# Reading the bank of product 7 at its own product, and holding back the first loads

## The chip, the cores and the metric

The kernel runs on one core of a Trainium2 chip. The metric is the device time of one execution in microseconds (us). Before the change it is 2088.18 us, the median of 3 runs (2087.85 to 2088.67). The engines are called by the profile's names: PE (matrix multiply, with PEld for its weight loads), DVE (vector), ACT (scalar), POOL (GpSimd) and SP (which here only issues DMA transfers; "SPq" is its queue).

## The reference

One layer of a streaming encoder, for a prompt of 2048 tokens and a sample of 32 tokens that share the weights. Cut to what matters here:

```python
def layer(x, pool_hist, n_valid, S0, ...):
    h = rmsnorm(x, g_pre_mix)
    z = h @ w_in                                  # 1024 -> 2560 columns
    u, zq, zf, zi, zg = jnp.split(z, [...], axis=-1)
    ...                                           # pooling mixer and gated recurrence
    x = x + rmsnorm(y_mix, g_post_mix)
    h2 = rmsnorm(x, g_pre_ffn)
    f = (jax.nn.silu(h2 @ w_gate) * (h2 @ w_up)) @ w_down   # 1024 -> 2816 -> 1024
    return x + rmsnorm(f, g_post_ffn), new_pool, S1
```

The changed places are the very first product, `zi = h @ w_in[:, COL_I:]` of the first half of the prompt (the "values"), and the two products with `w_gate` and `w_up`.

## The kernel before, in words

The prompt is worked in two halves of 1024 tokens (`halves`). Every float32 operand of a large product is split into a rounded part "hi" and a rest "lo", and a product is three matmuls (hi*hi, hi*lo, lo*hi) of 128 x 128 weights with 512 columns; all of them are issued by line 199.

**The start.** `first_values` (line 566) runs with all engines in written order. The contraction over 1024 channels is cut into 8 blocks k of 128. For each block two things are loaded: the channels of x (tile `xT`, 128 x 512 floats, 256 KB per block) and the rows of `w_in` (tile `wrow`, 256 KB per block). Both come through SP's one queue, in the order of the code: x of block 0 in two halves around w 0, then w 1, x 1, then x 2 and 3 as one transfer (512 KB), w 2 and 3 as one, and so on to block 7, then the constants (`cons`), four token tiles `xt` of 512 KB (line 451), and more. Nothing holds these issues back but the queue itself. ACT and DVE split each block: ACT `xg` (line 600) and DVE `xg` (601) for x, ACT `whw` (612, 615, 236) and DVE `wlw` (614, 616, 237) for w; then PE does 12 matmuls for the block into four banks `vps`. Behind block 5 PE does the matmuls `rb<-dg` that spread the scale of the tokens; `dg` comes from the four token tiles through ACT (line 319, sum of squares), POOL (325, 326) and DVE (461).

**Gate and up.** `gate_up` (1246) computes the two products block by block in seven products of a Winograd-like 2 x 2 scheme (`step`, 1353). For each m (even: a block of `w_gate`, odd: one of `w_up`; 22 in each half) there are two accumulation banks: `M.x` takes products 1, 6, 5, 3 and `M.y` takes products 7 and 4. So product 4 adds into the bank that product 7 has filled, and the quantity c22 needs `M.y` as it stands after 7 and before 4, and `M.x` as it stands after 5 and before 3. ACT copies `M.x` into c22 behind product 5 (line 1393; for m = 4 and 5, which are not "held", DVE adds, line 1395), and `rest` (1402), run at the start of the next slot, has DVE add `M.y` (line 1403). `order_of` gives the slots: mostly (m,1), (m-1,4), (m-1,3), (m,6), (m,2), (m,7), (m,5); for the last two, a and b, it ends (a,7), (b,7), (a,5), (b,5), (a,4), (b,4), (a,3), (b,3). The weights are prepared some slots ahead (`advance`, 1431), and `hidden` (1201) splits finished results and stores them.

Then comes the product with `w_down` (`down`), whose tail ends the program.

Of the kernel before, what the change touches and what calls it, by code (L numbers as in the profile page):

```python
# [13 lines left out]
ALU = mybir.AluOpType  # L14
PSUM = bass.MemoryType.PSUM

P = 128
# [61 lines left out]
def body(tc, ins, outs, cst):  # L79
    nc = tc.nc  # L80
    ctx = ExitStack()
    with ctx:
# [9 lines left out]
        def ztile(name, shape=None, dt=F32):  # L92
            return UP.tile(shape or [P, SLOT], dt, tag="u", name=name)
# [13 lines left out]
        def t2(name, shape=None, dt=F32):  # L107
            return TP.tile(shape or [P, 512], dt, tag="t", name=name)
# [7 lines left out]
        x_t = ins["x_channels"].rearrange("(k p) t -> p k t", p=P)  # L116
        w_in = ins["w_in"][0]
# [154 lines left out]
        def raws(n):  # L272
            its = Stream.items
            while Stream.nraw < min(n, len(its)):
                its[Stream.nraw] = its[Stream.nraw]()
                Stream.nraw += 1
# [146 lines left out]
        COL_Q, COL_F, COL_I, COL_G = 512, 1024, 1536, 2048  # L423
# [19 lines left out]
        def channel_load(S, tg, k, n):  # L443
            t0 = S.tok0 + tg * 512
            nc.sync.dma_start(out=S.xT[tg][k // 2][:, k % 2:k % 2 + n], in_=x_t[:, k:k + n, t0:t0 + 512])
# [52 lines left out]
        def scaled_channels(S, tg):  # L498
            if S.B:
                rb = S.rb[tg]  # L500
            else:
                rb = axbank("rb")
                for i in range(4):
                    mm(rb[:, i * P:(i + 1) * P], ones, S.dg[tg][:, i], True, True, 112.0)
            if S.hT is None:
                S.hT = [(xtile(f"hThi{k}"), xtile(f"hTlo{k}")) for k in range(KD)]
            cs = slice(tg * 512, tg * 512 + 512)
            yield 0.0
            for k in range(0, KD, 2):
                x = S.xT[tg][k // 2]  # L510
                for i in range(2):
                    nc.vector.scalar_tensor_tensor(x[:, i], x[:, i], g_pre[:, k + i:k + i + 1], rb, ALU.mult, ALU.mult)
                    nc.scalar.copy(S.hT[k + i][0][:, cs], x[:, i])
                for i in range(2):
                    hi, lo = (t[:, cs] for t in S.hT[k + i])
                    nc.vector.tensor_tensor(lo, x[:, i], hi.bitcast(F32), ALU.subtract)
                S.seen[tg] = k + 2
                if S.B and tg == 0 and k >= 4:
                    ahead(Stream.used + k // 2 - 1)
                yield 5000.0 if S.B and tg == 0 else 2800.0  # L520
# [45 lines left out]
        def first_values(S):  # L566
# [7 lines left out]
            front_loads(S)  # L574
            S.xT[0] = [ztile("xT", [P, 2, 512]) for _ in range(4)]
            for kp in range(4):
                if kp:
                    channel_load(S, 0, 2 * kp, 2)
                    raws(kp + 1)
                    continue  # L580
                x0 = x_t[:, 0, S.tok0:S.tok0 + 512]
                nc.sync.dma_start(out=S.xT[0][0][:, 0, 0:256], in_=x0[:, 0:256])
                raw = ztile("wrow", [P, 2 * 512])
                Stream.items[0] = lambda: raw
                for i in range(2):
                    nc.sync.dma_start(out=raw[:, i * 512:(i + 1) * 512], in_=w_in[i * P:(i + 1) * P, COL_I:COL_I + 512])
                    if i == 0:
                        nc.sync.dma_start(out=S.xT[0][0][:, 0, 256:512], in_=x0[:, 256:512])
                    else:
                        channel_load(S, 0, 1, 1)  # L590
                raws(1)
# [18 lines left out]
            raw = Stream.items[0]  # L610
# [12 lines left out]
            for k in range(0, KD, 2):  # L623
# [9 lines left out]
                for kk in range(2):  # L633
# [9 lines left out]
                    if k + kk == KD - 3:  # L643
                        later = scaled_channels(S, 1)
# [601 lines left out]
        def gate_up(S, on_last):  # L1246
# [8 lines left out]
            jobs, later, gs = [], [], {}  # L1255
# [55 lines left out]
            def product(M, p, ps, start):  # L1311
                while p not in S.F:
                    S.post[1].step()
                wf, F = M.f.pop(p), S.F[p]
                for k in (0, 2):
                    trios = [(*(wf[:, i, kk * P:(kk + 1) * P] for i in range(2)),
                              *(x[:, (kk % 2) * 512:(kk % 2) * 512 + 512] for x in F[kk // 2])) for kk in (k, k + 1)]
                    for n, (a, b) in enumerate(in_turn(trios)):
                        mm(ps, a, b, start and k == 0 and n == 0, k == 2 and n == 5, rcost(512), not start)
                        if n % 3 == 2:  # L1320
                            poll()

            def close(M, name):
                c = getattr(M, name)
                if M.gate is None:
                    later.append(lambda: nc.scalar.activation(c, c, AF.Silu))
                else:
                    nc.vector.tensor_tensor(c, c, getattr(M.gate, name), ALU.mult)
# [24 lines left out]
            def step(m, p):  # L1353
                M = mats[m]
                if p == 1:
                    M.gate = mats[m - 1] if m % 2 else None
                    M.x = mmbank("gx") if M.held else axbank("gw")
                    product(M, 1, M.x, True)
                    M.c11 = t2("c11")
                    nc.scalar.copy(M.c11, M.x)  # L1360
                    if not M.held:
                        M.p1, M.c11 = M.c11, t2("c11")
                elif p == 2:
                    if M.held:
                        z = axbank("gz")
                        product(M, 2, z, True)
                        nc.vector.tensor_tensor(M.c11, z, M.c11, ALU.add)
                        close(M, "c11")
                    else:
                        product(M, 2, M.x, False)  # L1370
                        if M.gate is None:
                            nc.scalar.activation(M.c11, M.x, AF.Silu)
                        else:
                            nc.vector.tensor_tensor(M.c11, M.x, M.gate.c11, ALU.mult)
                elif p == 6:
                    if not M.held:
                        M.x = mmbank("gx")
                    product(M, 6, M.x, not M.held)
                    M.c21 = t2("c21")
                    if M.held:  # L1380
                        nc.scalar.copy(M.c21, M.x)
                    else:
                        nc.vector.tensor_tensor(M.c21, M.x, M.p1, ALU.add)
                    if m == len(mats) - 1:
                        sampled([m - 1, m])
                elif p == 7:
                    M.y = axbank("gy")
                    product(M, 7, M.y, True)
                elif p == 5:
                    product(M, 5, M.x, False)  # L1390
                    M.c22 = t2("c22")
                    if M.held:
                        nc.scalar.copy(M.c22, M.x)
                    else:
                        nc.vector.tensor_tensor(M.c22, M.x, M.p1, ALU.add)
                    if m < LEAD:
                        if m % 2:
                            sampled([m - 1, m])
                    elif m < len(mats) - 2 and m % 2 == 0:
                        sampled([m, m + 1])  # L1400

                    def rest():
                        nc.vector.tensor_tensor(M.c22, M.y, M.c22, ALU.add)  # L1403
                        close(M, "c22")
                    later.append(rest)
                elif p == 4:
                    product(M, 4, M.y, False)
                    nc.vector.tensor_tensor(M.c21, M.y, M.c21, ALU.add)
                    close(M, "c21")
                else:  # L1410
                    product(M, 3, M.x, False)
                    M.c12 = t2("c12")
                    src = M.x
                    if not M.held:
                        src = M.c12
                        nc.vector.tensor_tensor(M.c12, M.x, M.p1, ALU.add)
                        M.p1 = None
                    if M.gate is None:
                        nc.scalar.activation(M.c12, src, AF.Silu)
                    else:  # L1420
                        nc.vector.tensor_tensor(M.c12, src, M.gate.c12, ALU.mult)
                        jobs.append(hidden(S, m // 2, [M.c11, M.c12, M.c21, M.c22]))
                        mats[m - 1] = mats[m] = None
# [62 lines left out]
        class Down:  # L1486
            w = [None] * len(GROUPS)
# [308 lines left out]
```

## Time and profile before

| | before |
|---|---|
| median of 3 runs | 2088.18 us |
| profiled execution, its own time | 2086.21 us |
| its span, first to last instruction | 2084.4 us |
| PE busy | 2071.4 us (99%) |
| DVE, ACT, POOL busy | 68%, 40%, 14% |
| granted TensorE clock (mean of the core) | 0.998 |

The span is what the profile's rows cover; the profiled execution's own time is 1.8 us longer. A row of the timeline reads: start and length in us, engine, line, operation, tile written <- tiles read, shape, how many were merged, and in brackets how long the engine had been idle and what ended that.

### The profile page before, as it was taken

Reading aid. Unit: us, or ns where it says so; the run is one execution under the profiler, and the core shown is the slowest. Engines: PE = TensorE matmul, PEld = TensorE weight load, DVE = VectorE, ACT = ScalarE, POOL = GpSimd, SP = SyncE. Lnnn points to the kernel's source line nnn. Section 1 sums busy time; section 2 is a strip of 40 time slices with the busy share of each in tenths; the row PEclk is TensorE's granted clock in tenths of the full one; section 3 lists DMA queues with packets and bytes.
Section 4 is the critical chain, followed back from the end, with each engine's and each line's share of the span. In section 5 each row is a group of like instructions: output and inputs, shape, how many; then the busy total and the mean of one; then the engine's idle time right before and its main releaser. Section 6 shows DMA issues by size and latency. Waiting matters only on the chain.

```text
span 2084.4 us, 34134 instructions
## 1 busy us (share of the span) xinstructions
PE 2071.4 (99%) x13112; PEld 1689.0 (81%) x13112; DVE 1423.6 (68%) x2303; ACT 830.7 (40%) x1661; POOL 281.9 (14%) x387
## 2 busy tenths in 40 slices
PE   9999999999999999999999999999999999999998
PEld 8788888888888888788888788888888778888876
DVE  6566765787776778365575697776666766566587
ACT  6444445654444445233334563444444521011032
POOL 1133302100000000122231200000000210110133
PEclk9999999999999999999999999999999999999999
DMA  9321144435555558211014614554445796776778
GB/s 326 112 72 52 45 142 144 150 115 174 157 162 147 158 171 262 72 46 36 25 54 174 202 50 138 163 149 144 142 138 171 237 326 208 216 225 207 213 225 213
DMA packets 393361, 321.06 MB, mean 154 GB/s; under 512 B 18128, under 2 KB 320720, under 8 KB 393200
## 3 DMA queue, kind: packets, MB, share of 16 engines
q1 hardware_dynamic: 390752, 310.98, 48.1%
q0 software_dynamic: 2016, 7.34, 1.9%
q8 instruction: 103, 1.69, 0.3%
q10 hardware_dynamic: 432, 0.57, 0.1%
q14 instruction: 58, 0.48, 0.1%
HBM read 218.36 MB, written 100.47 MB: 153 GB/s over the span
## 4 chain that ended last, share of the span: by engine, by line
PE 94%; DVE 3%; issue 1%; ACT 1%; DMA 0%; POOL 0%; SPq 0%; DVEq 0%; POOLq 0%; ACTq 0%
PE gx L199 22%; PE mmb L199 16%; PE gy L199 11%; PE dx L199 10%; PE ops L199 10%; PE gz L199 5%; PE dy L199 5%; PE vps L199 4%; PE dz L199 3%; PE gb L199 1%; PE gw L199 1%; PE gsps L199 1%; DVE acc L1581 1%; PE ups L199 1%; PE tps L342 1%
## 5 line engine op out<-in xcount | busy, mean ns | idle before, releaser
L199 PE MATMUL gx<-fhi,wf 128*128 128x512 f32 x1376 | 387.0, 391 | 0.0
L199 PEld LDWEIGHTS gx<-fhi,wf 128*128 128x128 f32 x1376 | 256.7, 188 | 55.0 <-issue 2.2
L199 PE MATMUL gx<-flo,wf 128*128 128x512 f32 x688 | 213.1, 390 | 0.0
L199 PE MATMUL gy<-fhi,wf 128*128 128x512 f32 x704 | 201.6, 390 | 1.0 <-DVE c L1403 1.0
L199 PE MATMUL dx<-dhi,hst 128*128 128x512 f32 x640 | 185.3, 391 | 1.0 <-DVE acc L1581 0.9
L199 PE MATMUL mmb<-hTlo,whi 128*128 128x512 f32 x512 | 176.3, 405 | 0.0
L199 PE MATMUL mmb<-hThi,whi 128*128 128x512 f32 x512 | 165.8, 405 | 0.0
L1581 DVE TENSOR_TENSOR acc<-dx,acc 128x512 f32<-128x512 f32 x168 | 115.0, 689 | 71.3 <-PE dx L199 70.3
L199 PE MATMUL mmb<-hThi,wlo 128*128 128x512 f32 x512 | 159.0, 392 | 0.0
L1301 DVE TENSOR_TENSOR wf<-s,wf 128x512 fp32r<-128x512 f32 x176 | 119.7, 687 | 56.1 <-ACT wf L1296 54.2
L199 PEld LDWEIGHTS gy<-fhi,wf 128*128 128x128 f32 x704 | 131.8, 188 | 29.1 <-DVE c L1403 1.4
L199 PEld LDWEIGHTS gx<-flo,wf 128*128 128x128 f32 x688 | 129.1, 188 | 27.0
L1296 ACT CAST wf<-s 128x512 fp32r<-128x512 f32 x176 | 107.9, 621 | 102.3 <-DVE s L1277 31.5
L199 PEld LDWEIGHTS dx<-dhi,hst 128*128 128x128 f32 x640 | 119.6, 188 | 30.2 <-issue 3.4
L1520 ACT CAST dhi<-t 128x1024 fp32r<-128x1024 f32 x20 | 20.7, 1053 | 250.7 <-DVE dlo L1521 182.4
L1301 DVE TENSOR_TENSOR wf<-wraw,wf 128x512 fp32r<-128x512 f32 x132 | 89.6, 686 | 34.4 <-ACT wf L1296 34.4
L199 PEld LDWEIGHTS mmb<-hTlo,whi 128*128 128x128 f32 x512 | 96.2, 188 | 20.8 <-issue 1.3
L199 PEld LDWEIGHTS mmb<-hThi,wlo 128*128 128x128 f32 x512 | 96.3, 188 | 19.3 <-issue 0.7
L1296 ACT CAST wf<-wraw 128x512 fp32r<-128x512 f32 x132 | 80.7, 621 | 76.0 <-PE gx L199 36.3
L199 PEld LDWEIGHTS mmb<-hThi,whi 128*128 128x128 f32 x512 | 91.8, 188 | 21.1 <-issue 3.8
L199 PE MATMUL gy<-flo,wf 128*128 128x512 f32 x352 | 108.7, 389 | 0.0
L199 PE MATMUL dx<-dlo,hst 128*128 128x512 f32 x320 | 98.7, 389 | 0.0
(333 smaller groups left out, 3995.0 us busy)
## 6 DMA issues: line engine op xcount, KB each, us to landing
hst<-hdFalse SPq DMA_DIRECT2D x140, 256.0 KB, 2.9
hst<-hdTrue SPq DMA_DIRECT2D x140, 256.0 KB, 2.9
wraw<-in_w_gate_dram SPq DMA_DIRECT2D x50, 512.0 KB, 4.0
wraw<-in_w_up_dram SPq DMA_DIRECT2D x50, 512.0 KB, 4.0
hdFalse<-hhi SPq DMA_DIRECT2D x77, 256.0 KB, 2.3
hdFalse<-hlo SPq DMA_DIRECT2D x77, 256.0 KB, 2.3
hdTrue<-hhi SPq DMA_DIRECT2D x77, 256.0 KB, 2.6
hdTrue<-hlo SPq DMA_DIRECT2D x77, 256.0 KB, 2.6
```

The lines of the kernel that those rows point to most:

```text
L199: nc.tensor.matmul(out, l, r, start=start, stop=stop, skip_group_check=more)
L342: nc.tensor.transpose(ps[:, c:c + P], xn[:, (2 * kp + kk) * P:(2 * kp + kk + 1) * P], ident)
L1296: nc.scalar.copy(wf[:, 0], getattr(M, src) if isinstance(src, str) else src)
L1301: nc.vector.tensor_tensor(wf[:, 1], getattr(M, src) if isinstance(src, str) else src, wf[:, 0].bitcast(F32), ALU.subtract)
L1520: nc.scalar.copy(hi, src)
L1581: nc.vector.tensor_tensor(dst, ps, dst, ALU.add)
```

## The change

Two edits that do not touch each other. At the start the loads of block pairs are held back: x 2 and w 2, and x 3 and w 3, become four transfers of 256 KB. Before x 2 is issued, POOL copies one column of w 0 into the place that x 2 will fill, so that the transfer has to wait until w 0 has landed and POOL has run; before x 3 it does so from w 1; and before x 4 and 5 from x 1. All stand in SP's one queue, so what is behind them waits too.

In `step` the bank `M.y` is read into c22 at product 7 (ACT copy, or DVE add for m = 4 and 5), and at product 5 DVE adds `M.x` to it. `rest` is gone; only `close` (activation or multiplication) is left for the next slot.

```diff
             for kp in range(4):
+                if kp == 1:
+
+                    raw = ztile("wrow", [P, 2 * 512])
+                    Stream.items[1] = lambda: raw
+                    seen = Stream.items[0][:, 0:1], Stream.items[0][:, 512:513]
+                    for i in range(2):
+                        x, w = S.xT[0][1][:, i], raw[:, i * 512:(i + 1) * 512]
+                        nc.gpsimd.tensor_copy(x[:, 0:1], seen[i])
+                        nc.sync.dma_start(out=x, in_=x_t[:, 2 + i, S.tok0:S.tok0 + 512])
+                        nc.sync.dma_start(out=w, in_=w_in[(2 + i) * P:(3 + i) * P, COL_I:COL_I + 512])
+                    raws(2)
+                    continue
                 if kp:
+                    if kp == 2:
+                        nc.gpsimd.tensor_copy(S.xT[0][2][:, 0, 0:1], S.xT[0][0][:, 1, 0:1])
                     channel_load(S, 0, 2 * kp, 2)
                     raws(kp + 1)
                     continue
@@
                 elif p == 7:
                     M.y = axbank("gy")
                     product(M, 7, M.y, True)
+                    M.c22 = t2("c22")
+                    if M.held:
+                        nc.scalar.copy(M.c22, M.y)
+                    else:
+                        nc.vector.tensor_tensor(M.c22, M.y, M.p1, ALU.add)
                 elif p == 5:
                     product(M, 5, M.x, False)
-                    M.c22 = t2("c22")
-                    if M.held:
-                        nc.scalar.copy(M.c22, M.x)
-                    else:
-                        nc.vector.tensor_tensor(M.c22, M.x, M.p1, ALU.add)
+                    nc.vector.tensor_tensor(M.c22, M.x, M.c22, ALU.add)
...
-
-                    def rest():
-                        nc.vector.tensor_tensor(M.c22, M.y, M.c22, ALU.add)
-                        close(M, "c22")
-                    later.append(rest)
+                    later.append(lambda: close(M, "c22"))
```

## Rows read from the trace of the kernel before

**Rows 1.** The page, busy time, share of the span and instructions of each engine.

```profile
PE 2071.4 (99%) x13112; PEld 1689.0 (81%) x13112; DVE 1423.6 (68%) x2303; ACT 830.7 (40%) x1661; POOL 281.9 (14%) x387
```

**Rows 2.** Waits of PE, whole span: us in total, times, longest.

```profile
PE gy L199 <- DVE c L1403: 1.0, 1, 1.0
PE dx L199 <- DVE acc L1581: 0.9, 2, 0.7
```

**Rows 3.** Busy time by stage: stretch, length, busy us (instructions) of each engine.

```profile
5.26:8.98 3.72, 3.40 (x12) 2.48 (x12) 1.77 (x4) 1.70 (x3) 0.00 (x0) 1.00 0.92 289
8.98:9.77 0.79, 0.73 (x2) 0.30 (x2) 0.74 (x1) 0.11 (x1) 0.00 (x0) 1.00 1.07 412
...
384.00:770.00 386.00, 386.00 (x1720) 319.34 (x1719) 298.68 (x463) 187.63 (x326) 6.41 (x12) 1.00 0.50 148
1190.00:1640.00 450.00, 449.02 (x2623) 370.33 (x2622) 333.72 (x518) 208.02 (x369) 20.87 (x20) 1.00 0.48 144
```

**Rows 4.** The chain that ended last, first 60 us: start, us, what.

```profile
2.58 5.61 DMA xT<-x_channels
...
9.77 13.56 PE vps L199 x58
...
24.52 24.50 PE vps L199 x108
```

**Rows 5.** Timeline near the end of gate and up, second half.

```profile
1625.65 0.57 ACT L1393 COPY c<-gx 128x512 f32<-128x512 f32 x1
...
1628.06 0.63 PE L199 MATMUL gx<-fhi,wf 128*128 128x512 f32 x2
...
1628.94 0.68 DVE L1403 TENSOR_TENSOR c<-gy,c 128x512 f32<-128x512 f32 x1
...
1629.67 0.73 PE L199 MATMUL gy<-fhi,wf 128*128 128x512 f32 x2 [0.98 <-DVE c L1403]
```

**Rows 6.** Groups by line: count, busy us, mean ns, idle before and who ended it.

```profile
L199 PE MATMUL gx<-fhi,wf 128*128 128x512 f32 x1376 | 387.0, 391 | 0.0
...
L1403 DVE TENSOR_TENSOR c<-gy,c 128x512 f32<-128x512 f32 x44 | 30.3, 688 | 26.8 <-ACT c L1393 26.7
```

**Rows 7.** Timeline of the first 17 us, ACT, PE and SP.

```profile
1.17 0.42 SPq L586 DMA_DIRECT2D wrow<-in_w_in_dram  x1
...
5.26 2.48 PE L199 MATMUL vps<-whw,xg 128*128 128x512 f32 x8
...
6.07 0.62 ACT L615 CAST whw<-wrow 128x512 fp32r<-128x512 f32 x1 [0.45 <-DMA wrow<-in_w_in_dram]
...
8.21 0.72 ACT L600 ACTIVATE xg<-xT,cons 128x512 fp32r<-128x512 f32 x1 [1.52 <-DMA xT<-x_channels]
...
9.66 0.72 ACT L600 ACTIVATE xg<-xT,cons 128x512 fp32r<-128x512 f32 x1 [0.73 <-DMA xT<-x_channels]
...
16.13 1.14 ACT L236 CAST whw<-wrow 128x512 fp32r<-128x512 f32 x2 [0.23 <-DMA wrow<-in_w_in_dram]
```

**Rows 8.** DMA issues: count, KB each, median us to landing (first 1.5 us; whole span).

```profile
wrow<-in_w_in_dram SPq DMA_DIRECT2D x1, 256.0 KB, 3.4
...
hst<-hdFalse SPq DMA_DIRECT2D x140, 256.0 KB, 2.9
```

**Rows 9.** Timeline, one POOL operation without and with DVE at work beside it.

```profile
23.11 0.55 POOL L326 TENSOR_TENSOR st<-st,nhalf 128x1 f32<-128x1 f32 x1
...
2067.59 1.42 DVE L1612 SCALAR_TENSOR_TENSOR acc<-acc,st,gv 128x512 f32<-128x512 f32 x2 [0.57 <-POOL st L326]
...
2068.55 0.86 POOL L326 TENSOR_TENSOR st<-st,nhalf 128x1 f32<-128x1 f32 x1
```

**Rows 10.** Timeline, from the token tiles to the matmuls behind block 5.

```profile
21.60 1.06 ACT L319 ACTIVATE junk<-xt 128x1024 bf16<-128x1024 f32 x1
...
23.69 0.29 DVE L461 TENSOR_SCALAR dg<-cons,st 128x128 f32<-128x128 f32 x1 [0.96 <-POOL st L326]
...
24.03 0.30 PEld L199 LDWEIGHTS rb<-dg,ones 128*128 128x128 f32 x2 [0.23 <-DVE dg L461]
```

## The prediction

> **What bounds the kernel now.** I read the page's busy times first, then the waits of PE, then a table by stage, then the start and the one stall of gate and up in the timeline. PE is busy 2071.4 of 2084.4 us [rows 1], so an edit can only pay where PE stands still: 13 us in all. The waits of PE show how little of that has a name: one wait of 1.0 us on DVE's line 1403, and two on line 1581 in the product with `w_down` (0.9 us, not touched) [rows 2]. By stage, the first half's gate and up has PE busy 386.00 of 386.00 us and the second half's 449.02 of 450.00 [rows 3]: there the missing 0.98 us is that one wait. Whatever the first edit does to DVE and ACT elsewhere, PE has nothing to gain from it there. In the start, the chain that ends last runs through the landing of x 1 (2.58 + 5.61 = 8.19 us), then PE alone from 9.77 [rows 4]. So there are two places, about 1 us each.
>
> **Gate and up.** Per block m, nothing is added or removed: before, one ACT copy (of `M.x`, at product 5) and one DVE add (of `M.y`, one slot later); after, one ACT copy (of `M.y`, at product 7) and one DVE add (of `M.x`, at product 5). The DVE add stands at the same place in DVE's order, since nothing is issued between the end of a slot's step and the start of the next. What moves is who holds which bank. Before, product 4 could not start into `M.y` until DVE's add, late in DVE's queue, had read it; after, until ACT's copy, issued two or more slots earlier, has.
>
> The stall: the last gx matmul before it starts at 1628.06 + 0.63 - 0.39 = 1628.30 (two merged, one lasts 0.39 [rows 6]), the next, product 4 of a, at 1629.67, after line 1403 ran 1628.94 to 1629.62 [rows 5]. That is 1.37 us, where a matmul follows the one before it in 24.50 / 108 = 0.227 us [rows 4]: 1.14 us lost, of which 0.98 counts as idle. The slots just ahead of it are (a,7), (b,7), (a,5), (b,5). ACT's copies for a and b now belong to the first two, and ACT had come as far as the copy of (a,5) by 1625.65 [rows 5], so both would be done some 2 us before 1628.5. I take all of it: **-1.1 us**. Bounds: 0 if ACT is late after all, and +0.6 if ACT's copy, 0.57 us, came in front of a weight cast that PE waits for. What is late next: product 3 into `M.x` now waits for the DVE add instead of an ACT copy, but two slots of 12 x 0.227 = 2.7 us lie between. In the other 43 blocks the edit also ends a DVE wait on the ACT copy (26.7 us in all [rows 6]); it costs nothing now, because PE was busy throughout, and returns nothing. c22 is taken from its pool a slot earlier; a wait for a free buffer would stall ACT's copy, and the weights are prepared four slots ahead (10.9 us of PE), which I count as cover: 0.
>
> **The start, what the wait costs now.** From 5.26 to 9.77 PE starts 14 matmuls [rows 3]; at 0.227 us they need 3.18 us, so 4.51 - 3.18 = 1.33 us are lost. Of these, 0.5 are in the first eight (2.48 us instead of 7 x 0.227 + 0.39 = 1.98 [rows 7]), which no transfer held up. The other 0.8 us are block 1: ACT waited 1.52 us for x 1 [rows 7]. w 0 lands at 1.17 + 3.4 = 4.57 [rows 7, 8], before any held-back transfer could have moved, so the first matmul at 5.26 stays where it is.
>
> **What holding back does.** x 1 was issued at 2.58 and took 5.61 us, against 2.9 for 256 KB at the median [rows 4, 8]. If all its excess is the company of the 512 KB transfers behind it, it lands near 6.3; if none, at 8.19. I take 7: then ACT's `xg` of block 1 is no longer late and PE runs through from 5.26, 0.8 us ahead of before.
>
> POOL's copy of one column: the trace has no such copy. Its bounds are 0 and 0.55 us, the longer one-column operation [rows 9]; I take 0.2. Then x 2 is issued at about 4.57 + 0.3 = 4.9 (before: right behind x 1) and lands at 4.9 + 2.9 = 7.8, w 2 half a microsecond of issue later at 8.3. Before, x 2 and 3 landed at 9.66 and PE still had work; so blocks 2 and 3 are in time. SP has nothing else queued that anyone waits for soon. POOL's next work is the token statistics, past 19 us.
>
> But PE cannot keep the 0.8 us by itself. Behind block 5 it meets `rb<-dg`, and there it already waits 0.23 us for the last `dg` [rows 10]. That `dg` hangs on the last token tile (ACT 21.60, DVE 23.69), ACT's work before that on the landing of w 6 and 7 at 16.1, where ACT waited [rows 7], and that on every byte queued before it: from 8.98 us the transfers run at 412 GB/s with every DMA engine busy (share 1.07 [rows 3]). So the start gains only what the whole stream gains. Before, the stream ran at 289 GB/s from 5.26 to 8.98 [rows 3]: 3.72 x (1 - 289/412) = 1.1 us lost. After, that loss may shrink, but a gap is added, from x 1's end to the first bytes of x 2 at about 4.9 + 2.9 - 0.65 = 7.1 (256 KB at 412 GB/s are 0.65). With x 1 at 6.3 the gap is 0.8 and the net gain 0.3; with x 1 at 8.19 there is neither. I take **-0.3 us**; bounds -0.8 (PE's share) and +1.6 (rival 2).
>
> On the price of a gate the row and a page meet. The row: 2.9 us from issue to landing for 256 KB, of which 0.65 are bytes, so 2.2 are paid whenever nothing is queued ahead [rows 8]. The Trainium skill, "DMA: Bandwidth & Descriptors", section "Anatomy of one DMA — SWDGE (gpsimd) path", gives a fixed 2.0 us plus bytes at 436 GB/s for transfers issued from GpSimd, which makes 2.6 us as an estimate; the trace, of one issued from SP, agrees within 0.3. By the page the first bytes of x 2 come at 6.9 instead of 7.1, and the sum would be -1.6. The rule speaks against the change: each gate exposes a fixed part that a full queue had hidden.
>
> A second rule could lengthen the gate. The same one-column POOL operation takes 0.55 us, and 0.86 where DVE runs an operation with two SBUF inputs beside it [rows 9]. The Trainium skill, "SBUF — State Buffer", section "SBUF: two separate sides", says that these two share a port pair which one of them holds for a whole instruction. The trace agrees in sign; here it would add about 0.3 us to the first gate, and the sum would be -1.1.
>
> **The sum.** -1.1 - 0.3 = -1.4 us. The profiled execution's own time is 2086.21 (span 2084.4 and 1.8 around it); it becomes 2084.8. The median of the runs shown is 2.0 above the profiled one, so the forecast there is 2088.18 - 1.4 = 2086.8.
>
> **Rivals.** (1) Holding back does not do what it says: x 1 is late by itself, by its own packets, and lands near 8.2 as before. For it: ACT waited for w 1 too, until 6.07 [rows 7], when little of the later load can have moved. Against it: x 1 took twice as long as an ordinary 256 KB. The start gives 0, the sum -1.1: 2087.1.
> (2) Slower: the gates starve the stream. Place: the third gate, x 4 and 5 behind x 1. If x 1 lands at 8.19, POOL runs after a DVE operation (0.7, half of 1.42 [rows 9]) and takes 0.2, the issue is at 9.1 and its first bytes at 11.3, while what is queued (x 2 to w 3, 4 x 0.65 = 2.6 us from 8.2) ends at 10.8: 0.5 us idle, and a second slow stretch like the 289 GB/s one costs its 1.1 again. Then w 6 and 7, the last `dg` and PE are 1.6 us later: -1.1 + 1.6 = +0.5, 2088.7. It decides the sign from a delay of 1.1 us on.
> (3) The wait in gate and up is replaced, not removed: ACT's copy of `M.y` sits behind ACT's backlog and product 4 waits for it just as long. Against it: ACT was 2 us ahead there. Only the start is left: -0.3, 2087.9.
>
> **How the numbers follow.** Forecast 50%, rival 1 23%, rival 2 15%, rival 3 12%. The times lie between 2086.8 and 2088.7; the forecast's own bound on the start (-0.8) reaches 2086.3. With the spread of the runs shown (0.8 us) and the unknown costs (+0.6 in gate and up) the range is 2085.4 to 2089.0. A measurement of this kernel tells 0.2%, 4.2 us, from no change. No case reaches it: 4.2 us faster would take a third of all PE idle time, and 4.2 slower a stall that no row suggests, such as a wait for buffers. I leave 3% to each, 94% to within 0.2%.
>
> **What would show it.** Right: PE's waits no longer name the add of c22, and second-half gate and up is busy to the last 0.1 us; ACT's `xg` of block 1 starts by about 7 us; the wait at `rb<-dg` grows from 0.23 to about 0.7, because PE comes earlier than `dg` does. Wrong: ACT still waits for x 1 until 8 us (rival 1); w 6 and 7 land past 17 us and `rb` starts past 25 (rival 2); product 4 near the end waits for ACT (rival 3); any new wait of PE in gate and up.

## The result, and the profile after

| | before | after |
|---|---|---|
| median of 22 runs each | 2087.86 us | 2091.20 us |
| range of the runs | 2085.81 to 2090.14 | 2087.82 to 2093.64 |
| profiled execution, its own time | 2086.21 us | 2090.33 us |
| its span | 2084.4 us | 2088.4 us |

The change makes the kernel slower: ratio 1.0016, 95% interval [1.001, 1.0022], some 3.3 us. That lies above the range of the prediction (2085.4 to 2089.0), though inside the 0.2% that was called no change.

First the waits of PE in the changed kernel, the view of [rows 2] (us in total, times, longest):

```profile
PE rb L199 <- DVE dg L461: 2.4, 3, 1.0
...
PE gb L199 <- ACT f_t L879: 0.8, 3, 0.4
PE vps L199 <- ACT va L714: 0.6, 1, 0.6
```

The wait for c22 is gone. Two stand there that were not in the list before: `rb<-dg` at the start, 2.4 us in three waits, and `vps<-va` in the second half (`gb<-f_t` was there, with 0.5 us). The prediction had let the last wait at `rb<-dg` grow from 0.23 to 0.7, but at no cost, since PE was to come earlier; `vps<-va` it did not have.

Next the start. The timeline of the changed kernel, ACT, POOL and SP (answers to [rows 7] and [rows 9]):

```profile
4.62 0.18 POOL L584 COPY xT<-wrow 128x1 f32<-128x1 f32 x1 [3.62 <-DMA wrow<-in_w_in_dram]
4.83 0.33 SPq L585 DMA_DIRECT2D xT<-x_channels  x1
...
6.03 0.75 POOL L584 COPY xT<-wrow 128x1 f32<-128x1 f32 x1 [1.23 <-DMA wrow<-in_w_in_dram]
6.05 0.68 DVE L628 TENSOR_TENSOR wlw<-wrow,whw 128x512 fp32r<-128x512 f32 x1
6.63 0.72 ACT L614 ACTIVATE xg<-xT,cons 128x512 fp32r<-128x512 f32 x1
...
6.71 0.67 POOL L591 COPY xT<-xT 128x1 f32<-128x1 f32 x1
6.80 0.33 SPq L585 DMA_DIRECT2D xT<-x_channels  x1
...
7.71 0.38 SPq L445 DMA_DIRECT2D xT<-x_channels  x1
...
17.73 0.62 ACT L236 CAST whw<-wrow 128x512 fp32r<-128x512 f32 x1 [0.21 <-DMA wrow<-in_w_in_dram]
...
23.43 1.06 ACT L319 ACTIVATE junk<-xt 128x1024 bf16<-128x1024 f32 x1 [0.29 <-DMA xt<-in_x_prompt_dram]
...
25.52 0.29 DVE L461 TENSOR_SCALAR dg<-cons,st 128x128 f32<-128x128 f32 x1 [1.15 <-POOL st L326]
...
25.86 0.50 PEld L199 LDWEIGHTS rb<-dg,ones 128*128 128x128 f32 x2 [1.14 <-DVE dg L461]
```

Read it from the top. Gate one opens at 4.8. ACT's `xg` of block 1 starts at 6.63 with no wait, where it stood until 8.21 before: x 1 was indeed held up by its company, the 512 KB transfers behind it. But gate two opens only when w 1 has landed and POOL has run, so x 3 is issued at 6.80, and x 4 and 5, behind it in SP's queue, at 7.71; before, all of these had been issued by 4.5. From there the delay runs along the stream: w 6 and 7 are used at 17.73 instead of 16.13, the last token tile at 23.43 instead of 21.60, and the last `rb` starts at 25.86 instead of 24.03 [rows 10], 1.83 us late, after a wait of 1.14 instead of 0.23.

The bytes show where the stream lost them. Busy time by stage, 5 to 13 us, of the kernel before and then of the changed one (last columns: granted clock, DMA share, GB/s):

```profile
5.00:13.00 8.00, 7.62 (x30) 5.31 (x29) 4.73 (x9) 4.71 (x9) 0.00 (x0) 1.00 0.99 346
```
```profile
5.00:13.00 8.00, 8.00 (x36) 6.38 (x35) 4.14 (x8) 4.08 (x8) 1.36 (x2) 1.00 0.81 253
```

8 us x (346 - 253) GB/s = 0.74 MB; at the 0.41 MB/us that a full queue moves [rows 3] this is 1.8 us, the delay of the last `rb`. PE is busy all the time in this stretch, and that hides the loss: PE is 1.4 us ahead of before by 12.7, and at `rb` it gives that back and loses 1.8 more.

Then a cost that the prediction did not have. The stage behind the last `rb`, changed kernel:

```profile
25.61:29.02 3.41, 3.16 (x9) 2.58 (x10) 2.47 (x5) 1.45 (x3) 0.00 (x0) 0.50 1.05 408
```

For 3.41 us the granted clock is 0.50 (1.2 of 2.4 GHz). The stretch begins within the last of the three waits of PE for `dg`, 2.4 us together. (The last 4 to 7 us of every profiled execution, the one before too, are at half the clock as well; here and below, a fall of the clock means one at the start.)

PE's matmuls come in the same order in both profiled executions, so each can be set against its counterpart. The difference of the starts, after less before:

```
last rb            +1.83     822 us (vps<-va)      +4.36
end of slow clock  +3.28     825 us                +4.71
91 us (wmr)        +3.51     1207 us (tps)         +5.28
137 us (gb<-f_t)   +3.75     1630 us (gy, c22)     +4.22     end +4.01
```

So the start makes +3.3, 0.5 follows soon after, the stretch from 822 to 1207 makes another +1.5, and the bank edit's own place gives 1.06 back. The steps at 91 us (0 to 0.9) and at 1207 (0 to 0.8) also stand in profiles of kernels whose code is the old one there, so one profile can't charge them to the change; the steps at 822 and 825 are another matter, as the experiments show.

### The profile page after: what moved, and what is told of

Same layout as the page of the kernel before. It is cut to its first block, busy times and chain, and to the rows that moved or that the text cites. A ratio compares the mean times of both kernels' runs of the same rounds, so it can differ in the third digit from the quotient of the medians.

```text
span 2088.4 us, 34131 instructions
## 1 busy us (share of the span) xinstructions
PE 2073.3 (99%) x13112; PEld 1690.0 (81%) x13112; DVE 1422.0 (68%) x2303; ACT 829.0 (40%) x1661; POOL 282.0 (14%) x390
## 4 chain that ended last, share of the span: by engine, by line
PE 92%; DVE 4%; DMA 2%; ACT 1%; issue 1%; POOL 1%; SPq 0%; DVEq 0%; POOLq 0%; ACTq 0%
PE gx L199 22%; PE mmb L199 16%; PE gy L199 11%; PE dx L199 10%; PE ops L199 10%; PE dy L199 5%; PE gz L199 5%; PE dz L199 3%; PE vps L199 2%; PE gb L199 1%; PE gw L199 1%; PE gsps L199 1%; PE ups L199 1%; DVE acc L1592 1%; DMA xT<-x_channels 1%
```

## The experiments

All times are medians of 11 runs, with those of the kernel before on the same chip beside them (33 runs; 27 in the last group); its medians there were 2087.74, 2088.42 and 2087.70. The ratio and its interval are estimated from all the runs, and the ratio is not exactly the quotient of the two medians. "Last rb" and the GB/s of 5 to 13 us are of the one profiled execution (24.03 and 346 in the kernel before, 25.86 and 253 in the changed one).

| kernel | time | before | ratio, interval | last rb | GB/s |
|---|---|---|---|---|---|
| bank edit only | 2087.14 | 2087.74 | 1.0000 [0.9992, 1.0009] | 24.23 | 345 |
| loads only | 2091.89 | 2087.74 | 1.0016 [1.0007, 1.0025] | 25.65 | 258 |
| split, no gates | 2088.01 | 2087.74 | 1.0000 [0.9991, 1.0009] | 26.48 | 323 |
| gate one only | 2087.40 | 2087.74 | 0.9999 [0.9991, 1.0008] | 23.97 | 313 |
| gate three only | 2089.76 | 2088.42 | 1.0005 [0.9996, 1.0014] | 24.93 | 277 |
| gates one and two | 2090.47 | 2088.42 | 1.0009 [1.0, 1.0018] | 26.25 | 242 |
| waits filled | 2089.97 | 2088.42 | 1.0009 [1.0, 1.0018] | 25.47 | 263 |
| bank edit, second half | 2087.41 | 2088.42 | 0.9996 [0.9987, 1.0004] | 24.30 | 344 |
| gate one + that | 2086.54 | 2087.70 | 0.9997 [0.9988, 1.0006] | 26.14 | 287 |
| changed kernel again | 2091.59 | 2087.70 | 1.0022 [1.0014, 1.0031] | 25.64 | 265 |
| waits filled again | 2089.55 | 2087.70 | 1.0011 [1.0002, 1.002] | 26.29 | 240 |

**Each edit alone.** The bank edit (the hunks of `step` in the diff):

> The bank edit alone, the loads as before. Theory (the held-back loads cost about 4 us, the bank edit gives back 1.1): 1.1 us faster than the kernel before, PE's wait for the c22 add near the end of gate and up is gone, no new wait of PE at the start. Rival (the bank edit brings waits of its own, such as the 0.6 us wait for the copy of va at 826 us seen after the change): same time as before or up to 0.8 us slower, with that wait in the trace.

and the loads (the hunks of `first_values`):

> The held-back loads alone, the bank read as before. Theory: 4 to 5 us slower than before; the last matmuls rb<-dg start near 25.9 us instead of 24.0, the granted clock falls to half for some 3.4 us behind them. Rival: 3.3 us slower, the whole of what the changed kernel lost, because the bank edit gives nothing.

The loss is the loads'. Alone they cost as much as the full change (4.2 us by the medians, 3.3 by the ratio); in the profiled execution the clock did not fall, against the expectation, and the last `rb` is 1.62 us late. The bank edit removes its stall, as expected, and yet is worth nothing that can be measured. Its trace shows why it need not be: a new wait of PE, at a place with nothing of c22:

```profile
822.14 0.58 ACT L700 COPY va<-vps 128x512 f32<-128x512 f32 x1
...
822.77 0.73 PE L199 MATMUL vps<-whw,hThi 128*128 128x512 f32 x2 [0.58 <-ACT va L700]
```

ACT's copy was at 818.79 before. Backwards from there: ACT waits for DVE's `xT`, DVE for a channel load. This is DVE's line 512 in the bank edit and, below it, in the kernel before:

```profile
807.10 1.42 DVE L512 SCALAR_TENSOR_TENSOR xT<-xT,cons,rb 128x512 f32<-128x512 f32 x2 [4.76 <-DMA xT<-x_channels]
```
```profile
804.39 1.42 DVE L512 SCALAR_TENSOR_TENSOR xT<-xT,cons,rb 128x512 f32<-128x512 f32 x2 [3.07 <-DMA rb<-roots]
```

Behind the start, only PE's order is written out by hand; the other engines' instructions are put in order by the framework's planner. PE's order is the same in both kernels. DVE's, ACT's and SP's differ from about 427 us, in the first half's gate and up, to 1635, also far behind the edited instructions: of the second half's channel loads SP issues one at 795.79 and three from 800.95 on before, and all four from 800.95 on with the edit.

**The bank edit where it can't disturb what follows.** In the first half the old code, in the second (`S.B`) the new; `bank(M, ps)` makes c22 from the bank `ps`, by ACT's copy or, for m = 4 and 5, DVE's add:

```diff
                     product(M, 7, M.y, True)
+                    _ = S.B and bank(M, M.y)
                 elif p == 5:
                     product(M, 5, M.x, False)
-                    M.c22 = t2("c22")
-                    if M.held:
-                        nc.scalar.copy(M.c22, M.x)
+                    if S.B:
+                        nc.vector.tensor_tensor(M.c22, M.x, M.c22, ALU.add)
                     else:
-                        nc.vector.tensor_tensor(M.c22, M.x, M.p1, ALU.add)
+                        bank(M, M.x)
...
                     def rest():
-                        nc.vector.tensor_tensor(M.c22, M.y, M.c22, ALU.add)
+                        _ = S.B or nc.vector.tensor_tensor(M.c22, M.y, M.c22, ALU.add)
```

> The bank edit in the second half alone, the loads as before. If what the bank edit gives back (0.6 to 0.8 at 822 us and 0.2 to 0.4 near 1207) comes from the planner placing the other engines' instructions differently after the first half's gate and up: nothing is lost ahead of 1190 us, the stall at 1629.67 goes, and the time is 1.0 to 1.1 us under before (2086.7 where before has 2087.7). If the losses at 822 and 1207 are chance or belong to the edit itself: the same time as the bank edit in both halves (2087.6).

1.0 us under before in the median, as expected; the interval still holds no change. One part of the expectation failed: its profiled execution did lose time ahead of 1190 us (0.7 at 91 and 0.7 at 1058) and 0.6 at 1207, all ahead of the first instruction that the edit moves (1235). The step at 1207, which the expectation had put down to the planner, stands in kernels without any bank edit too, so it need not come from the edit.

At 822 the traces say more: a loss of 0.7 to 1.7 there, and 0.35 at 825, stands in all five profiled executions with the full bank edit, and in none of the eight without it in the first half. So the edit in the first half brings the loss, in a place where it changes no instruction but, through the planner, the order. That the order carries it is argued from the traces, by way of the channel load; no run keeps the edit and restores the order, and which of the moved instructions matters is not shown.

**How much there was to win.** The c22 wait can be looked up in the profiles of the kernels that keep the old bank code. Waits of PE with loads unsplit, split without gates, gate one only, gates one and two:

```profile
PE gy L199 <- DVE c L1403: 1.0, 1, 1.0
```
```profile
PE gy L199 <- DVE c L1413: 0.7, 1, 0.7
```
```profile
PE gy L199 <- DVE c L1416: 0.4, 1, 0.4
```
```profile
PE gy L199 <- DVE c L1415: 1.4, 1, 1.4
```

(the first is that of [rows 2]). With gate three only, and with the loads alone, there is no such line. The order of PE, DVE and ACT is the same in these six, so the wait is a matter of how the engines happen to stand: 0 to 1.4 us, 0.6 on average, and 1.0 in the profile before.

**Splitting without gates.** Four transfers of 256 KB instead of two of 512, no POOL copy; against the changed loads (and, below it, gate one only):

```diff
-                    seen = Stream.items[0][:, 0:1], Stream.items[0][:, 512:513]
...
-                        nc.gpsimd.tensor_copy(x[:, 0:1], seen[i])
...
-                    if kp == 2:
-                        nc.gpsimd.tensor_copy(S.xT[0][2][:, 0, 0:1], S.xT[0][0][:, 1, 0:1])
```
```diff
-                        nc.gpsimd.tensor_copy(x[:, 0:1], seen[i])
+                        if i == 0:
+                            nc.gpsimd.tensor_copy(x[:, 0:1], seen[i])
...
-                    if kp == 2:
-                        nc.gpsimd.tensor_copy(S.xT[0][2][:, 0, 0:1], S.xT[0][0][:, 1, 0:1])
```

> The loads of blocks 2 and 3 as four transfers of 256 KB but with nothing to wait for. Theory (the waits starve the stream): within 0.5 us of before, token tiles and rb as before (24.0 us). Rival (smaller transfers are the cost): 3 us or more slower, rb past 25 us.

0.3 us over before: the split costs nothing that these runs can measure (to within 0.9 in 1000). Its profiled execution, the slowest of its eleven, is no test of the expectation that `rb` stays at 24.0: x 1 came late, PE waited 1.8 us for it, then the clock was at half, and `rb` started at 26.48, PE itself being late and not `dg`:

```profile
11.38:14.79 3.41, 3.41 (x10) 2.66 (x9) 2.85 (x5) 2.22 (x4) 0.00 (x0) 0.50 1.06 409
```

**Which gate.** First, gate one only (the second diff above):

> Only the first of the three waits is kept: x 2 behind w 0; x 3, w 3 and x 4 follow at once. Theory A (the gap is made by the first wait, nothing is queued between x 1's end at 6.6 and 7.1 us): most of the loss stays, rb near 25.3 us and 2 to 4 us slower than before. Theory B (the gap is made by the second wait, whose copy POOL could only run behind DVE, 0.75 us instead of 0.18): rb within 0.5 us of 24.0, within 0.7 us of before.

The time shows no loss. x 2 is issued at 4.82, and x 3, w 3, x 4 follow at once (5.67, 6.15, 6.62). The stream still moves 0.26 MB less by 13 us, yet the last `rb` is not later:

```profile
23.97 0.49 PE L199 MATMUL rb<-dg,ones 128*128 128x128 f32 x2 [0.76 <-DVE dg L461]
```

This is the forecast's start as drawn: ACT's `xg` of block 1 is 1.4 us early, PE is 0.8 us ahead by 12.4, and its weight load waits 0.95 for `dg` instead of 0.23. So it cannot pay. Next, gate three alone, put into the kernel before:

```diff
                 if kp:
+                    if kp == 2:
+                        nc.gpsimd.tensor_copy(S.xT[0][2][:, 0, 0:1], S.xT[0][0][:, 1, 0:1])
                     channel_load(S, 0, 2 * kp, 2)
```

> The kernel before with the third gate alone: x 4 and 5 wait for the landing of x 1; x 2 and 3 go in one 512 KB transfer as before. Theory A (each gate that leaves less in flight than its own issue, fixed time and copy take starves the stream, whichever gate it is): x 1 lands near 8.2, x 4 and 5 are issued at 8.4 to 9.1 instead of 4.06, about 5 us late; 1 MB is in flight then (until about 10.8), the first bytes come near 11, the stream runs slow after the gap, the last rb starts 0.7 to 1.2 us later than before (24.03) and the time is 2088.4 to 2089.0. Theory B (the second gate alone does the harm): x 4 and 5 come in time, rb as before to 0.3 us, time within 0.3 us of before.

Here is rival 2's picture. x 1 lands at 8.19, and SP goes on at 8.41:

```profile
8.19 0.19 POOL L579 COPY xT<-xT 128x1 f32<-128x1 f32 x1 [7.20 <-DMA xT<-x_channels]
```
```profile
8.41 0.37 SPq L445 DMA_DIRECT2D xT<-x_channels  x1
```

The last `rb` is 0.90 late, inside theory A's 0.7 to 1.2. The time is 1.3 over before's median on that chip, a little more than A's (0.6 to 1.2 over the 2087.8 it was written against); the interval holds no change. Then both of the others without the third (the changed loads less the two lines of gate three):

> The loads of the change with gates one and two, without the third and without the bank edit. Theory B: the whole delay is gate two's (x 3 and w 3 wait for w 1): x 4 and 5 stand behind w 3 in SP's order and are issued at 7.4 to 7.7 with or without the third gate, so nothing comes back: last rb at 25.6 to 25.9, time 2091 to 2092, as with the loads alone (2091.9). Rival (the third gate does it): rb near 24.0 and 2087.5, as with the first gate alone.

`rb` is 2.22 late with gate three gone: in the changed kernel the third gate costs nothing that shows, since SP is busy with x 3 and w 3 until 7.6 anyway, as theory B has it. That gate two alone does the harm is not so in general: gate three does some where it is the one that holds. (Gate two without gate one was not run.) The time is 2.0 over before, at 2090.47 under the 2091 to 2092 expected. The delay goes with the bytes that are late:

| | MB less than before, 5 to 13 us | at 0.41 MB/us | last rb later by |
|---|---|---|---|
| waits filled again | 0.85 | 2.1 us | 2.26 |
| gates one and two | 0.83 | 2.0 us | 2.22 |
| all three (changed) | 0.74 | 1.8 us | 1.83 |
| loads only | 0.70 | 1.7 us | 1.62 |
| waits filled | 0.66 | 1.6 us | 1.44 |
| changed kernel again | 0.65 | 1.6 us | 1.61 |
| gate three only | 0.55 | 1.3 us | 0.90 |
| gate one + bank edit, second half | 0.47 | 1.2 us | 2.11 |
| gate one only | 0.26 | 0.6 us | -0.07 |

In the six profiles with gate two the delay is that of the bytes to within 0.25 us, and below that some of it is free. The last row but one does not fit (see the end of this section): a late stream is not all that can make `rb` late. POOL's slow second copy adds little: in the kernel with the loads alone it took 0.24 us, not 0.75, x 3 went out at 6.56 instead of 6.80, and `rb` came 0.21 earlier.

**The clock.** Into the changed kernel, idle matmuls in PE's waits, ahead of the second to fourth token tile's `rb`:

```diff
+                    for _ in range(3 if tg and i else 0):
+                        mm(rb[:, i * P:(i + 1) * P], ones, ones, True, True, 0.0)
```

> The changed kernel with nine idle matmuls (128 columns, of ones, result not used) put in PE's waits between the first four rb transposes. If PE's standing still there is what lets the granted clock fall afterwards: clock 1.0 throughout from 9 us on, rb last at 25.8 to 26.0 as in the changed kernel, and about 1.3 us of its loss gone (2089.9 against 2091.2). If the clock falls for another reason: the same 3.4 us at half the clock, 2091.2 or up to 0.3 more.

The clock stays at 1.0 through the start; `rb` comes at 25.47, 0.39 earlier than in the changed kernel's profile and 1.44 later than before. The time is 1.6 over before on its chip, where the changed kernel had been 3.3 over on its own. To compare them on one chip, both ran again:

> The changed kernel once more, beside the next one on one chip: 2.8 to 3.6 us over before, with the granted clock at half after the rb matmuls.

> The changed kernel with PE's rb waits filled by idle matmuls, on the same chip. If the fall of the clock is what the filling saves: 1.0 to 1.6 us under the changed kernel. If the first measurement owed it to the chip: the same as the changed kernel to 0.4 us.

The filled kernel is 2.0 us faster by the medians, more than the 1.6 expected at most (2.1 by the means, almost three times its standard error of 0.8). The changed kernel's second profile, of the fastest of its eleven runs, had no fall of the clock:

```profile
25.64:29.02 3.38, 3.38 (x16) 2.85 (x17) 2.79 (x4) 1.98 (x3) 0.00 (x0) 1.00 1.05 407
```

Of the six profiled executions in which PE stood still for 1.8 us or more at the start, three had the 3.41 us at half the clock (changed, split without gates, gates one and two) and three had not, the longest total (2.7 us) among them. So a fall costs some 1.5 us (what PE loses more than before in the two executions that had it behind `rb`), in some executions.

How often it strikes can be read from the mean granted clock on record for every run, to three digits. In the ten profiles without a fall this mean is 0.9983 to 0.9991, in the three with it 0.9979 to 0.9981. So a run at 0.999 had none, one at 0.997 had more time at half the clock than any profile shows, and at 0.998 it can't be told. Runs, and their mean time:

| kernel | at 0.999 | at 0.998 | at 0.997 |
|---|---|---|---|
| before (the 93 runs beside the experiments) | 61, 2087.7 us | 31, 2088.4 us | 1 |
| changed, both measurements | 9, 2089.4 us | 13, 2091.4 us | 11, 2093.0 us |
| filled, both measurements | 18, 2089.9 us | 4, 2091.1 us | 0 |

So the fall strikes the changed kernel in at least 11 and at most 24 of 33 runs. Without it the changed kernel is as fast as the filled one (over several chips), 1.7 us over before, about the delay of the last `rb`; by these numbers, what filling wins is what the clock takes.

**What is left to win.** Gate one, and the bank edit in the second half, the two diffs above together:

> What cost nothing of both edits, together: the first gate alone, and the bank edit in the second half alone. Theory: the bank edit's stall near 1630 goes, nothing is lost at 822 us, the last rb starts where it did (24.0): 0.5 to 1.1 us under before. Rival (the stall at 1630 is not there in most executions, and the first gate is worth nothing): the same time as before to 0.3 us.

The median is 1.16 under before, a little more than the theory's most (1.1), but the interval, 0.9988 to 1.0006, does not tell it from before. Its one profile shows a worse start than that of gate one alone. In it w 6 and 7 are used 0.7 us late; then the last token tile landed late by itself, for a reason that the trace doesn't show, and `rb` came at 26.14:

```profile
23.70 1.06 ACT L319 ACTIVATE junk<-xt 128x1024 bf16<-128x1024 f32 x1 [1.52 <-DMA xt<-in_x_prompt_dram]
```

That execution was the slowest of its eleven; whether gate one sometimes makes `rb` late is open, the times of both kernels with it show no loss. No version alone beats the kernel before beyond doubt; the two with the bank edit in the second half only, taken together, lie 0.9 us under it in the mean (standard error 0.3), so a small gain is likely.

## Why the prediction was wrong

**The start, the step that failed: "After, that loss may shrink, but a gap is added".** The sum counted one gap, in front of x 2, and took 0.3 us as won (for an x 1 at 6.3, though its rows, 2.58 + 2.9, make 5.5, and PE's share was figured for 7; x 1 came by 6.6, so this is not what failed). Gate two was not priced at all: x 3 and w 3 wait for w 1, which lands at 6.0, so that behind x 1 only 512 KB are under way from 4.8 to 6.8 and x 4 comes out at 7.71. Measured: 253 GB/s instead of 346, `rb` 1.83 us late. The 2.2 us that "are paid whenever nothing is queued ahead" were in the text; they had to be set against what each gate leaves in flight, 0.5 MB or 1.2 us, gate by gate.

**Rival 2 (15%)** had the mechanism and the size: 1.6 us lost by a starved stream, with the signs "w 6 and 7 land past 17 us and `rb` starts past 25". Both came (17.73 and 25.86). It named the wrong gate, and tied it to an x 1 that lands at 8.19; x 1 landed by 6.6, as the likeliest case had it (near 7), and the stream starved all the same. Gate three alone did what the rival says, with `rb` 0.90 us late. The rival's 2088.7 is still 2.5 short of the measured 2091.2, by the next two points.

**Gate and up: "PE has nothing to gain from it there", "stands at the same place in DVE's order".** The stall went, at its place, by the 1.06 us that were forecast (1.1). But the order of DVE, ACT and SP changed from there to the end of the second half's gate and up, and PE lost about 1 us at 822 and 825 us; the edit alone in both halves measured no change where -1.1 stood. And the -1.1 was one draw of a wait that six profiles give 0.6 on average. Rival 3 named the right outcome, no gain, for a cause that did not occur: product 4 waited for nothing.

**Not in the prediction: the clock.** A wait of PE was priced at its length. Where the granted clock falls to half at its end or behind it, some 1.5 us come on top, in a third of the changed kernel's runs or more.

**Right:** the first matmul stays at 5.3; x 1's delay was its company, and ACT's `xg` of block 1 no longer waits; "PE cannot keep the 0.8 us by itself", since it meets `rb<-dg` anyway (shown by gate one only). **POOL's copy** took 0.18 us at gate one, beside a SCALAR_TENSOR_TENSOR of DVE, and 0.75 and 0.67 at the other two, beside TENSOR_TENSOR operations of 0.68 and 0.69; all three of DVE's have two SBUF inputs. Its bounds were 0 and 0.55, so two of the three lay above them. The Trainium skill, "SBUF — State Buffer", section "SBUF: two separate sides", says that the one that comes second is fully blocked for the other's instruction. The trace agrees for two copies of the three: they end at 6.78 and 7.38, just behind DVE's operations (6.73 and 7.35), some 0.5 us late where the prediction had 0.3 from [rows 9], though by the profile the first of them starts 0.02 before DVE's. It does not for the first copy: neither it nor DVE's operation beside it (0.48 us, as long as the next one, with no copy beside it) was held up.

## What to carry to other kernels

Before a transfer is held back until another lands, set what stays in flight against issue, wait and fixed time of the next; count that for every gate, in bytes, and look for the last consumer of the whole stream, not for the first matmul. Before an edit of one engine's work is priced by its own stall, ask who orders the other engines: where a planner does, the edit can move work far behind it, and the new order has a price too. And a stall of one microsecond in one profiled execution of a kernel whose runs spread over four is a sample, to be read from several.

## What the runs showed of the hardware

In the changed kernel the stream came back only slowly: 222 GB/s from 5 to 7 us, then 243, 216 and 330, and 395 from 13 to 15, though SP had issued 2.3 MB from 7.2 to 9.2; that is longer than the 2.2 us from an issue to its first bytes explain, and why is open. The clock at half came in stretches of 3.41 us in all three starts that had it; in two of them PE had stood still before it in waits of at most 1.0 and 1.2 us, with matmuls between them. The changed kernel's second profile has three such waits (0.8 us at most) and no fall.
